# Measured step costs in the planner of a two-layer RG-LRU / Gated DeltaNet trunk

## The chip, the core and the metric

The kernel runs on one core of a Trainium2 chip. The core has a matrix engine (TensorE, PE in the profile), a vector engine (VectorE, DVE), an activation engine (ScalarE, ACT), a general engine (GpSimd, POOL) and a queue that issues the transfers (SyncE, SP). Each engine works through its own list of instructions in order; semaphores hold an instruction until what it reads is there. The metric is the device time of one execution in microseconds; the median of several runs is quoted.

## The reference

A sequence of 2048 frames of width 1024 passes two layers and a final norm, all in 32-bit floats.

```python
c_act = silu(c)
for i in range(2):
    shift, scale, gate = split(c_act @ ada_w[i] + ada_b[i])
    h = rmsnorm(x, norm_g[i]) * (1 + scale) + shift
    out = rglru_block(h) if i == 0 else gated_deltanet_block(h)
    x = x + gate * out
return rmsnorm(x, final_g)

# rglru_block: proj = h @ in_w (1024 -> 2048), causal conv of 4 taps, two gates by 8 block matmuls
#   (128x128), log_a = -8 * r * softplus(-lam), b = sqrt(1 - a^2) * i * x, scan h_t = a_t h_{t-1} + b_t,
#   y = scan * silu(zg), out = y @ out_w
# gated_deltanet_block: proj = h @ in_w (q, k, v, z of 8 heads x 128, and a, b), conv of 4 taps and SiLU
#   on q, k, v, l2norm of q and k, then per head, in chunks:
#   T = (I + strict lower of (beta k k^T * decay))^-1
#   v_new = T (beta v) - T (beta k exp(g)) S;  o = (q exp(g)) S + attn v_new
#   S = S * e_last + k_dec^T v_new
#   o = rmsnorm(o) * silu(z), out = o @ out_w
```

## The kernel before

**Tiling.** Frames are taken in two units `u` of 1024, each in two tiles `i` of 512 (`TC`). The hidden activations lie with channels on partitions. Every large product keeps 32-bit precision with three fast passes: each factor is split into a rounded part and the rest (`hh`/`hl` for activations, `whi`/`wlo` for weights), and `hi*hi + hi*lo + lo*hi` is accumulated. One job (`job`, through `products`, L668) is thus 24 matmuls of 128x128 by 512 columns into one bank of PSUM; `mm` is the bank of such a job, `mmo` that of an output projection.

**Stages.** The stages follow one another with some overlap. By the first and last matmul of each in the trace, in microseconds of the span: layer 1's input projection of unit 0 from 36 to 265 and of unit 1 to 476, with the conv (`convolve`, L746 to L769), the gates (`gates_thread`, L798 to L849) and the scan beside it; layer 1's output projection to 668; layer 2's input projection of unit 0 to 1217 and of unit 1 to 1734, with the work of the heads beside it; then layer 2's output projection with the final norm. In unit 0 of each layer the low part of a weight panel is made on GpSimd (`panels_thread`, L650) and kept in HBM; in unit 1 it is read back (L637).

**Layer 2, head by head.** A job's result is copied out (`extend`, L730), filtered by one step on GpSimd (L997) and three on VectorE (`taps`, L718), passed through tanh (L1009) and a multiply (L1014) and becomes `kt`, `qt` or `vt`. TensorE then transposes `kt` (`pk`, L1135), forms `pkk` (L1169) and `pqk` (L1257). `inverses_thread` inverts the 32x32 diagonal blocks on VectorE with 31 pairs of dependent small steps (`ttmp`, L1292, and `tblk`, L1295); `levels_thread` puts the blocks together with small matmuls (`px`, `pr`, L1334 to L1373). `recurrence_thread` goes through 8 chunks of 128 frames a unit and head. Each chunk is a chain over three engines: `pp` (two products with the state, L1412 and L1413), `zt` on VectorE (L1421), `py` (L1429), `yt` on ScalarE (L1435), `pS` (L1441, L1442), `state` on VectorE (L1454), and then `pp` of the next chunk. PE fills the time between with matmuls of the projection jobs.

**What sets the order.** The order on every engine is written by a planner inside the kernel when it is built, the class `Weave`. Each piece of work is a Python generator (a thread) with a priority. Before each step it yields the engine that the step needs, how long the step takes and, if wanted, a latency until its result may be used; it also yields events and buffer slots to wait for. `run` keeps a clock for each engine (`free`), takes the thread whose next step can start first (ties by priority), writes that step's instructions, and moves the clocks on. The clocks are the planner's own estimates; the chip knows only the order that they lead to and the semaphores. The jobs of the projection have the last priority, 9, and recurrences the first, 0. Transfers have an estimated speed, and `MARGIN` (2.4 us) is added behind some of them. In the text below, "planned" means by these clocks.

```python
LAG = {"pe": 0.2, "act": 0.3, "dve": 0.3, "pool": 0.2}           # latency where a step gives none
STT, EV, CP, TR, MM, M4 = 0.665, 0.605, 0.48, 0.109, 0.2163, 0.218
...
    self.free[w[0]] = t + w[1]
    th.t = t + w[1] + (w[2] if len(w) > 2 else self.LAG[w[0]])
```

`MM` is the planned time of one 512-column matmul in layer 2 and in both output projections; the jobs of layer 1 are given 0.2275.

## Time and profile before

| What | Value |
|---|---|
| median of 3 runs | 1935.67 us (1934.42 to 1940.69) |
| span of the profiled execution | 1937.1 us |
| PE busy / DVE busy / ACT busy / POOL busy | 1844.0 / 1471.2 / 1048.2 / 654.8 us |
| mean granted clock of TensorE | 0.984 |

The span is the time from the first to the last instruction of one profiled execution; the page shows no other time of that execution, and its span is 1.4 us above the median of the runs. A line of a group of instructions names the source line, the engine, the operation, what is written and read, the count, the busy time and the mean duration. A line of a wait names who waited for whom, the time in total, how often, and the longest. In a table of stretches, "PE busy (x)" is busy time and number of instructions, "PEclk" the share of TensorE's full clock that was granted. `PEld` is the load of a matmul's weights.

### The profile page before, as it was taken

To read this page: it belongs to the slowest core of one execution; us is meant where nothing else is said; L and a number is where in the kernel's file an instruction comes from. 1 tells how busy PE (TensorE), PEld (TensorE's weight loads), DVE (VectorE), ACT (ScalarE), POOL (GpSimd) and SP (SyncE) were. 2 spreads that over 40 slices of the span, in tenths; PEclk is the share of its full clock that TensorE was granted. 3 is DMA by queue.
4 is the path that set the end of the run, shared out by engine and by line. 5 is a ranking of instruction groups with operands and counts; after the bars stand their busy time and mean duration, and the time that the engine had idled before them with its cause. 6 is when DMAs were issued, how large, how long until landed. Compare 5 with 4: busy or idle time off the path is not lost.

```text
span 1937.1 us, 31289 instructions
## 1 busy us (share of the span) xinstructions
PE 1844.0 (95%) x10286; PEld 1503.9 (78%) x10286; DVE 1471.2 (76%) x3175; ACT 1048.2 (54%) x2587; POOL 654.8 (34%) x1116
## 2 busy tenths in 40 slices
PE   6999999999899999898999999999999999999998
PEld 3787778878688877677787877788888888888887
DVE  6898998887544668869888896769777878886653
ACT  3666677667212345375565663565666656654321
POOL 3344542223100235345445543333332334411110
PEclk9999999999899999999999998999999999999999
DMA  8476746554578735446676565555365555687751
GB/s 320 116 219 189 223 138 220 175 167 138 169 204 236 208 106 145 128 111 160 166 186 141 138 158 150 149 156 158 102 163 143 140 140 139 155 246 207 230 161 66
DMA packets 511723, 322.77 MB, mean 167 GB/s; under 512 B 371268, under 2 KB 439236, under 8 KB 511560
## 3 DMA queue, kind: packets, MB, share of 16 engines
q1 hardware_dynamic: 511560, 320.77, 59.1%
q8 instruction: 81, 1.33, 0.3%
q14 instruction: 82, 0.67, 0.1%
HBM read 219.93 MB, written 100.73 MB: 166 GB/s over the span
## 4 chain that ended last, share of the span: by engine, by line
PE 61%; DVE 20%; DMA 6%; issue 4%; ACT 4%; SPq 3%; POOL 2%; DVEq 0%; POOLq 0%; ACTq 0%
PE mm L668 31%; PE mmo L668 16%; DVE xf L718 2%; DVE ttmp L1292 2%; DVE tblk L1295 2%; PE pg L807 1%; PE py L1429 1%; PE pp L1412 1%; PE pS L1442 1%; PE pqk L1257 1%; PE pS L1441 1%; PE pp L1413 1%; PE pkk L1169 1%; DVE xf L756 1%; DMA raw<-in_w 1%
## 5 line engine op out<-in xcount | busy, mean ns | idle before, releaser
L718 DVE SCALAR_TENSOR_TENSOR xf<-xe,cw_s,xf 128x512 f32<-128x512 f32 x288 | 224.9, 784 | 20.6 <-POOL xf L997 18.1
L650 POOL TENSOR_TENSOR wlo<-raw,whi 128x1024 fp32r<-128x1024 f32 x48 | 120.9, 2519 | 143.6 <-ACT whi L644 115.4
L1292 DVE TENSOR_TENSOR ttmp<-blk,tblk 128x60 f32<-128x60 f32 (+24 forms) x496 | 125.4, 253 | 16.6 <-DMA blk<-blk_d 5.4
L1295 DVE TENSOR_TENSOR tblk<-tblk,ttmp 128x60 f32<-128x60 f32 (+24 forms) x496 | 124.8, 252 | 10.7
L644 ACT CAST whi<-raw 128x1024 fp32r<-128x1024 f32 x96 | 100.2, 1044 | 50.3 <-DMA raw<-in_w 44.5
L668 PE MATMUL mmo<-oh,yh 128*128 128x512 f32 x256 | 102.1, 399 | 4.8 <-ACT oh L907 4.8
L668 PE MATMUL mm<-hh_('in2', 0)_5342,whi 128*128 128x512 f32 x256 | 105.3, 411 | 0.0
L668 PE MATMUL mm<-hh_('in2', 0)_5437,whi 128*128 128x512 f32 x256 | 105.3, 411 | 0.0
L668 PE MATMUL mmo<-ol,yh 128*128 128x512 f32 x256 | 102.2, 399 | 3.0 <-DVE ol L909 3.0
L668 PE MATMUL mm<-hh_('in2', 0)_5342,wlo 128*128 128x512 f32 x256 | 104.7, 409 | 0.0
L668 PE MATMUL mm<-hl_('in2', 0)_5343,whi 128*128 128x512 f32 x256 | 104.7, 409 | 0.0
L668 PE MATMUL mm<-hl_('in2', 0)_5438,whi 128*128 128x512 f32 x256 | 104.1, 407 | 0.0
L668 PE MATMUL mm<-hh_('in2', 1)_12030,wlo 128*128 128x512 f32 x256 | 104.1, 407 | 0.0
L668 PE MATMUL mm<-hl_('in2', 1)_12219,whi 128*128 128x512 f32 x256 | 104.0, 406 | 0.0
L668 PE MATMUL mm<-hh_('in2', 0)_5437,wlo 128*128 128x512 f32 x256 | 103.9, 406 | 0.0
L668 PE MATMUL mm<-hh_('in2', 1)_12218,whi 128*128 128x512 f32 x256 | 103.6, 405 | 0.0
L668 PE MATMUL mm<-hh_('in2', 1)_12030,whi 128*128 128x512 f32 x256 | 103.5, 404 | 0.0
L668 PE MATMUL mm<-hl_('in2', 1)_12031,whi 128*128 128x512 f32 x256 | 103.3, 403 | 0.0
L668 PE MATMUL mm<-hh_('in2', 1)_12218,wlo 128*128 128x512 f32 x256 | 103.2, 403 | 0.0
L668 PE MATMUL mmo<-ol,oh 128*128 128x512 f32 (+1 forms) x264 | 103.1, 391 | 0.0
L668 PE MATMUL mmo<-oh,ol 128*128 128x512 f32 (+1 forms) x264 | 103.1, 391 | 0.0
L668 PE MATMUL mmo<-oh,oh 128*128 128x512 f32 (+1 forms) x264 | 103.0, 390 | 0.0
(331 smaller groups left out, 5649.8 us busy)
## 6 DMA issues: line engine op xcount, KB each, us to landing
raw<-in_w SPq DMA_DIRECT2D x96, 512.0 KB, 4.2
araw<-in_ada_w SPq DMA_DIRECT2D x32, 512.0 KB, 4.3
xt<-x_d SPq DMA_DIRECT2D x32, 512.0 KB, 4.9
xt_d<-xb SPq DMA_DIRECT2D x192, 64.0 KB, 2.4
xk<-xt_d SPq DMA_DIRECT2D x24, 512.0 KB, 6.1
xt<-in_x SPq DMA_DIRECT2D x16, 512.0 KB, 4.4
ada<-in_ada_w SPq DMA_DIRECT2D x16, 512.0 KB, 8.5
y_d<-tz SPq DMA_DIRECT2D x32, 256.0 KB, 3.2
```

Source lines behind the costliest of these rows:

```text
L644: act.copy(hi, raw)
L650: pool.tensor_tensor(lo, raw, f(hi), ALU.subtract)
L668: pe.matmul(pt, lhsT=lhs[a][:, k, :], rhs=rhs[b][:, k, :], start=(k == 0 and n == 0), stop=(k == KT - 1 and n == 2))
L718: dve.scalar_tensor_tensor(xf, xe[:, 1 + j:1 + j + TC], wc[:, j:j + 1], xf, ALU.mult, ALU.add)
L756: dve.scalar_tensor_tensor(xf[:, 3:TC], pt[:, j:j + TC - 3], wc[:, j:j + 1], xf[:, 3:TC], ALU.mult, ALU.add)
L807: pe.matmul(pg, lhsT=a[:, g, :], rhs=b, start=(q == 0), stop=(q == 2))
L1169: pe.matmul(pkk[:, b, :], lhsT=kc, rhs=kc, start=True, stop=True)
L1257: pe.matmul(pqk[:, b, :], lhsT=kt[:, b * P:(b + 1) * P], rhs=qt[:, b * P:(b + 1) * P], start=True, stop=True)
L1292: dve.tensor_tensor(tmp, blk[:, j, j + 1:32].unsqueeze(2).to_broadcast([P, r, c_]), t[:, j, 0:c_].unsqueeze(1).to_broadcast([P, r, c_]), A ...
L1295: dve.tensor_tensor(t[:, j + 1:32, 0:c_], t[:, j + 1:32, 0:c_], tmp, ALU.subtract)
L1412: pe.matmul(pp[:, 0, :], lhsT=kc, rhs=S_, start=True, stop=True)
L1413: pe.matmul(pp[:, 1, :], lhsT=qc, rhs=S_, start=True, stop=True)
```

## The change

Only the planner's numbers and rules change; every step still issues the same instructions with the same operands, and no buffer, slot, event or priority is touched. On each engine the same instructions stand in another order; ScalarE alone has ten more loads of a function table, 63 for 53, which the build puts in where the function set changes from one instruction to the next. There are five parts.

1. **Durations.** Most steps get another duration, given as the distance from the start of one step to the start of the next on that engine.
2. **Latencies.** The latency behind a step becomes 0.2 us for PE, 0.128 for ScalarE, 0.113 for VectorE and 0.034 for GpSimd, in place of 0.2, 0.3, 0.3 and 0.2. Own latencies of steps (0.13, 0.27, 0.0 and others) go, apart from a few with `MARGIN`.
3. **Weights.** When a thread comes to PE from another engine or from a wait, and PE would otherwise go straight on, 0.12 us is added.
4. **Tables.** A step on ScalarE that needs the set of exp and tanh, or that of sqrt, names it; 1.28 us is added where the planner's present set is the other. Before, every sqrt was simply given 3.1 us.
5. **Steps that exclude each other.** A VectorE step marked `dve2` that would start while a GpSimd step marked `pool2` is planned to run starts when that one ends, and the reverse.

```diff
+LAG = {"pe": 0.2, "act": 0.128, "dve": 0.113, "pool": 0.034}
+WEIGHTS = 0.12
+TABLE = 1.28
+SHARED = {"dve2": "pool2", "pool2": "dve2"}
...
-    LAG = {"pe": 0.2, "act": 0.3, "dve": 0.3, "pool": 0.2}
...
+        self.held = {"dve2": [], "pool2": []}
+        self.table = "exp"
...
-        return max(th.t, self.free.get(w[0], 0.0))
+        free = self.free.get(w[0].rstrip("2"), 0.0)
+        if w[0] == "pe" and th.last != "pe" and th.t > free - 0.1:
+            return max(free, th.t + WEIGHTS)
+        return max(th.t, free)
+
+    def engine(self, th, t, kind, dur, lag=None, table=None):
+
+        e = th.last = kind.rstrip("2")
+        if table is not None and table != self.table:
+            t, self.table = t + TABLE, table
+        if kind in SHARED:
+            for a, b in self.held[SHARED[kind]][-6:]:
+                if a <= t < b:
+                    t = b
+            self.held[kind].append((t, t + dur + (0.08 if e == "dve" else 0.0)))
+        self.free[e] = t + dur
+        th.t = t + dur + (LAG[e] if lag is None else lag)
...
+            if t > th.t and not isinstance(w, tuple):
+                th.last = None
...
-                self.free[w[0]] = t + w[1]
-                th.t = t + w[1] + (w[2] if len(w) > 2 else self.LAG[w[0]])
+                self.engine(th, t, *w)
...
-    STT, EV, CP, TR, MM, M4 = 0.665, 0.605, 0.48, 0.109, 0.2163, 0.218
+    STT, EV, CP, TR, MM, M4 = 0.665, 0.605, 0.48, 0.109, 0.228, 0.224
...
-                    yield "pool", 2.3
+                    yield "pool2", 2.39
                     pool.tensor_tensor(lo, raw, f(hi), ALU.subtract)
...
-            yield "dve", STT, 0.13 if j < 3 else 0.27
+            yield "dve2", 0.663
             dve.scalar_tensor_tensor(xf, xe[:, 1 + j:1 + j + TC], wc[:, j:j + 1], xf, ALU.mult, ALU.add)
...
-        yield "dve", 0.7
+        yield "dve2", 0.599
         xl = tile_([P, TC], "xr", "xl", F32R)
...
-        yield "act", 3.1
+        yield "act", 0.54, LAG["act"], "sqrt"
         act.activation(tr, tr, AF.Sqrt, scale=-0.25)
...
-        yield "dve", EV
+        yield "dve2", 0.604
         r = tile_([P, TC], kind + "t", kind + "t")
...
-            dur = 0.065 + r * c_ / 960.0
-            yield "dve", dur, 0.13
+            dur = 0.075 + r * c_ / 960.0
+            yield "dve2", dur
...
-                    yield "dve", 0.27
+                    yield "dve", 0.265
                     zt = tile_([P, P], "zt", "zt")
...
-                yield "act", 0.16
+                yield "act", 0.18
                 yt = tile_([P, P], "yt", "yt")
...
-                yield "dve", 0.27
+                yield "dve", 0.258
                 if first:
                     dve.tensor_copy(out=S_, in_=pS[:, 0, :])
```

The other threads change in the same way. The built orders are compared below at three places; lines of the changed kernel are 17 higher than the same lines before.

The first place is on PE in layer 2, unit 0: the two transposes of `kt` (`pk`, four instructions each) that stand at 802 and 807 us of the profiled execution. Before, one matmul of a job stands between them:

```order
L668 MATMUL mm<-hl_('in2', 0)_5343,whi 128x512
L1135 MATMUL pk<-ident,kt 128x128 x4
L668 MATMUL mm<-hh_('in2', 0)_5342,wlo 128x512
L1135 MATMUL pk<-ident,kt 128x128 x4
L668 MATMUL mm<-hh_('in2', 0)_5437,whi 128x512
L668 MATMUL mm<-hl_('in2', 0)_5438,whi 128x512
```

Now the second of them stands here, thirty rows behind the first:

```order
L685 MATMUL mm<-hh_('in2', 0)_5455,whi 128x512
L685 MATMUL mm<-hl_('in2', 0)_5456,whi 128x512
L685 MATMUL mm<-hh_('in2', 0)_5455,wlo 128x512
L685 MATMUL mm<-hh_('in2', 0)_5455,whi 128x512
L685 MATMUL mm<-hl_('in2', 0)_5456,whi 128x512
L1380 MATMUL px_7011<-tf,ac 64x64 x8
L1152 MATMUL pk<-ident,kt 128x128 x4
L685 MATMUL mm<-hh_('in2', 0)_5455,wlo 128x512
```

Eleven matmuls of the next job and two sets of small products (`pr` and `px`) moved in between the two transposes.

The second place is on PE in layer 2, unit 1, inside the chain of chunks of one head. Before, `py` of a chunk is followed by four matmuls of a job, then `pS`, then five, then `pp` of the next chunk:

```order
L668 MATMUL mm<-hh_('in2', 1)_12030,wlo 128x512
L668 MATMUL mm<-hh_('in2', 1)_12030,whi 128x512
L668 MATMUL mm<-hl_('in2', 1)_12031,whi 128x512
L668 MATMUL mm<-hh_('in2', 1)_12030,wlo 128x512
L1441 MATMUL pS<-yt,kd 128x128
L1442 MATMUL pS<-yt,at 128x128
L668 MATMUL mm<-hh_('in2', 1)_12030,whi 128x512
L668 MATMUL mm<-hl_('in2', 1)_12031,whi 128x512
L668 MATMUL mm<-hh_('in2', 1)_12030,wlo 128x512
L668 MATMUL mm<-hh_('in2', 1)_12030,whi 128x512
L668 MATMUL mm<-hl_('in2', 1)_12031,whi 128x512
L1412 MATMUL pp<-state_106,kt 128x128
```

Now, for the same head:

```order
L1446 MATMUL py<-zt,ac 128x128
L685 MATMUL mm<-hh_('in2', 1)_12131,wlo 128x512
L685 MATMUL mm<-hh_('in2', 1)_12131,whi 128x512
L685 MATMUL mm<-hl_('in2', 1)_12132,whi 128x512
L1458 MATMUL pS<-yt,kd 128x128
L1459 MATMUL pS<-yt,at 128x128
L685 MATMUL mm<-hh_('in2', 1)_12131,wlo 128x512
L685 MATMUL mm<-hh_('in2', 1)_12131,whi 128x512
L685 MATMUL mm<-hl_('in2', 1)_12132,whi 128x512
L1429 MATMUL pp<-state_106,kt 128x128
```

One matmul of a job moved out of the first interval and two out of the second.

The third place is on ScalarE in layer 1, around one sqrt (L830 before, L847 now). Before:

```order
L752 COPY edge_123<-mm 128x3
L830 ACT_TABLE_LOAD
L830 ACTIVATE tg<-tg 128x512
L783 ACT_TABLE_LOAD
L783 ACTIVATE tz<-mm 128x512
L857 ACTIVATE tg<-pg,gb_s 128x512
```

Now:

```order
L769 COPY edge_123<-mm 128x3
L847 ACT_TABLE_LOAD
L847 ACTIVATE tg<-tg 128x512
L874 ACT_TABLE_LOAD
L874 ACTIVATE tg<-pg,gb_s 128x512 x2
```

The load after the sqrt now stands ahead of a gate's tanh rather than of the `z` path's. In all, 31 loads ahead of a sqrt stand there now, and 26 before.

Counted over PE's list in the same way: from the last matmul of a job to the `pg` that depends on it (layer 1, unit 0), the median distance is 61 matmul slots before and 99 now; from a `k` job to its `pk` in the second half of layer 2's unit 0, 52 before and 62 now; from a `q` job to its `pqk` there, 57 and 85. In layer 2's unit 1 the same two distances are 41 and 40, and 46 and 46. A slot is one 512-column matmul, or one small 32-bit product of 128 columns. In the chain of chunks the intervals from the first `pp` to `py`, from `py` to the first `pS` and from the first `pS` to the next `pp` were counted, in slots that stand between, the second product of a pair included. Of some 180 such intervals in unit 1, 2 had room for no more than three other matmuls before, and 51 have now; in unit 0, 12 of 150 before, and 64 now.

More of the change, by code (lines that the diff above doesn't have):

```diff
@@ L63, in __init__ @@
     def __init__(self, gen, prio, t):
-        self.gen, self.prio, self.t, self.want = gen, prio, t, None
+        self.gen, self.prio, self.t, self.want, self.last = gen, prio, t, None, None
 class Weave:
     SEEN = 0.92
-    LAG = {"pe": 0.2, "act": 0.3, "dve": 0.3, "pool": 0.2}
     def __init__(self):
         self.free = dict.fromkeys(("pe", "act", "dve", "pool", "sp", "dma"), 0.0)
+        self.held = {"dve2": [], "pool2": []}
+        self.table = "exp"
         self.threads = []
@@ L312, in first_small_thread @@
         w.set(ev("c"))
-        yield "dve", 1.57
+        yield "dve", 1.6
         for k in range(KT):
@@ L385, in columns_thread @@
         dve.tensor_scalar(sp2, sp2, 2.0, None, ALU.mult)
-        yield "act", 0.2
+        yield "act", 0.111, LAG["act"], "exp"
         act.activation(aexp, alog_s, AF.Exp)
-        yield "dve", 0.1
+        yield "dve", 0.085
         dve.tensor_scalar(aexp, aexp, -1.0, None, ALU.mult)
@@ L451, in scale_thread @@
         put("tt", ttok)
-        yield "pool", 0.75, MARGIN / 2 if late else 0.2
+        yield "pool", 1.2, MARGIN / 2 if late else 0.2
         rs = tile_([P, 1], "rs", "rs")
@@ L558, in split_thread @@
         ttok = yield slots[tag]
-        yield "act", 0.665
+        yield "act", 0.711
         h = tile_([P, TC], tag, "h")
@@ L683, in job @@
         pt = ps.tile([P, TC], F32, tag=bank, name="mm")
-        yield from products(pt, (hi, lo), h, (lambda k: ev("split", (name, i), k)), 0.2275 if layer == 1 else MM)
+        yield from products(pt, (hi, lo), h, (lambda k: ev("split", (name, i), k)))
         if all(q != p for q, _ in jobs[n + 1:]):
@@ L722, in extend @@
         if g == 0:
-            yield "pool", 0.1
+            yield "pool", 0.101
             pool.memset(xe[:, 0:4], 0.0)
@@ L726, in extend @@
             yield ev("carry", key, g - 1)
-            yield "pool", 0.14
+            yield "pool", 0.299
             pool.tensor_copy(out=xe[:, 0:4], in_=carry)
-        yield "act", CP
+        yield "act", 0.484
         act.copy(xe[:, 4:4 + TC], pt)
         put(bank, mtok)
-        yield "pool", 0.14, 0.0
+        yield "pool", 0.279
         pool.tensor_copy(out=carry, in_=xe[:, TC:TC + 4])
@@ L739, in convolve @@
     def convolve(xf, pt, mtok, wc, bias, edge, key, g, bank):
-        yield "act", 0.66 if bias is not None else 0.57, 0.0
+        yield "act", 0.681
         if bias is None:
@@ L795, in gates_thread @@
             w.set(ev("lasthalves"))
-        yield "act", CP
+        yield "act", 0.521
         xh = tile_([P, TC], "xh", "xh", F32R)
         act.copy(xh, xf)
-        yield "dve", 0.7
+        yield "dve2", 0.599
         xl = tile_([P, TC], "xr", "xl", F32R)
@@ L832, in gates_thread @@
             yield ev("hcar", n, u * NTC + i - 1)
[L833 removed]
+        yield "dve2", 0.603
         dve.tensor_tensor(ti, ti, tr, ALU.mult)
         put("tg", rtok)
[L836 removed]
+        yield "dve2", 1.19
         init = 0.0 if u + i == 0 else hcar[:, n:n + 1]
@@ L952, in residual1_thread @@
         row = yield ev("gate", 0, d)
-        yield "dve", EV
+        yield "dve", 0.616
         dve.tensor_tensor(pt, pt, row[:, d * TC:(d + 1) * TC], ALU.mult)
-        yield "dve", EV
+        yield "dve", 0.606
         dve.tensor_tensor(xr, pt, xr, ALU.add)
@@ L1187, in key_thread @@
         for b in range(TB):
-            yield "act", 0.295, 0.0
+            yield "act", 0.298
             act.activation(kd[:, b, :], kd[:, b, :], AF.Copy, scale=ec[:, b, P - 1:P])
-        yield "pool", 0.16
+        yield "pool", 0.343
         pool.tensor_tensor(nk, nk, rr, ALU.mult)
```

221 lines of the change are left out of this document (109 added, 112 removed).

## The prediction, as it was made before the run

> **What bounds the kernel now.** I read the busy times first, then the table of stretches, then what PE waits for in each stretch, and last the timeline around the longest wait.
>
> ```profile
> PE 1844.0 (95%) x10286; PEld 1503.9 (78%) x10286; DVE 1471.2 (76%) x3175; ACT 1048.2 (54%) x2587; POOL 654.8 (34%) x1116
> ```
>
> PE has 1937.1 - 1844.0 = 93 us without work. The change adds and removes no work on PE, so it can only move this idle time and the clock that goes with it. The stretches say where that is:
>
> ```profile
> core 0: us, PE busy (x) PEld busy (x) DVE busy (x) ACT busy (x) POOL busy (x), PEclk, DMA share, GB/s
> 60.00:270.00 210.00, 196.34 (x839) 156.65 (x837) 190.22 (x278) 139.24 (x210) 100.40 (x86) 0.98 0.64 188
> 270.00:490.00 220.00, 219.26 (x950) 176.53 (x950) 182.21 (x276) 156.60 (x215) 66.53 (x60) 0.99 0.55 171
> 490.00:720.00 230.00, 221.10 (x953) 175.76 (x952) 127.87 (x185) 62.01 (x98) 38.36 (x55) 0.98 0.64 183
> 720.00:1000.00 280.00, 257.02 (x1666) 212.97 (x1664) 225.51 (x550) 159.49 (x493) 132.92 (x241) 0.98 0.58 149
> 1000.00:1240.00 240.00, 222.78 (x1429) 182.87 (x1428) 198.53 (x537) 139.38 (x424) 109.21 (x186) 0.97 0.60 153
> 1240.00:1720.00 480.00, 477.10 (x3212) 398.65 (x3212) 371.76 (x1051) 293.18 (x927) 160.95 (x389) 1.00 0.57 146
> ```
>
> Layer 2's unit 0 (720 to 1240) leaves PE idle for 23.0 + 17.2 = 40.2 us; unit 1 (1240 to 1720), which does nearly the same per head, for 2.9. The granted clock is 0.98 and 0.97 in unit 0 and 1.00 in unit 1; if the missing clock were all lost, it would cost 0.02 x 280 + 0.03 x 240 = 12.8 us. Layer 1's unit 0 (60 to 270) has 13.7 us idle and 0.02 x 210 = 4.2 us of clock. What differs between the units of layer 2 is the GpSimd step that makes the low half of a weight panel, L650:
>
> ```profile
> 720.00:1000.00 280.00, 41.51 (x17) 0.98 0.58 149
> 1000.00:1240.00 240.00, 26.84 (x11) 0.97 0.60 153
> 1240.00:1720.00 480.00, 0.00 (x0) 1.00 0.57 146
> ```
>
> The timeline shows what it does to VectorE (three engines, each in its own order):
>
> ```profile
> 801.49 2.89 POOL L650 TENSOR_TENSOR wlo<-raw,whi 128x1024 fp32r<-128x1024 f32 x1 [3.40 <-ACT whi L644]
> ...
> 802.08 2.40 DVE L1292 TENSOR_TENSOR ttmp<-blk,tblk 128x75 f32<-128x75 f32 x1
> ...
> 805.32 0.23 DVE L1292 TENSOR_TENSOR ttmp<-blk,tblk 128x70 f32<-128x70 f32 x1
> ...
> 806.26 0.68 DVE L1014 SCALAR_TENSOR_TENSOR kt<-tt,xf 128x512 f32<-128x512 f32 x1
> ...
> 807.00 0.66 PE L1135 MATMUL pk<-ident,kt 128*128 128x128 f32 x4 [3.89 <-DVE kt L1014]
> ```
>
> A small step that takes 0.23 us when alone takes 2.40 while L650 runs, and ends with it. `kt` stands behind it in VectorE's list, and PE, which has `pk` next in its own, stands still for 3.89 us. The old planner had no rule for this. All waits of PE over 1.5 us in unit 0 of layer 2, and those of layer 1's unit 0 and of the switch to layer 1's output projection that matter (who waits for whom, us in total, times, the longest):
>
> ```profile
> PE pk L1135 <- DVE kt L1014: 7.6, 4, 3.9
> PE pp L1412 <- DVE state L1454: 6.4, 7, 1.8
> PE py L1429 <- DVE zt L1421: 5.3, 4, 1.9
> PE pqk L1257 <- DVE qt L1014: 3.3, 1, 3.3
> PE px L1334 <- DVE tf L1327: 3.3, 5, 1.6
> PE pqk L1257 <- DVE tblk L1295: 2.1, 1, 2.1
> PE px L1363 <- POOL rq L243: 2.1, 1, 2.1
> PE pqk L1257 <- DVE ttmp L1292: 1.9, 1, 1.9
> PE pS L1441 <- ACT yt L1435: 1.8, 2, 1.5
> PE pp L1412 <- DVE ttmp L1292: 1.6, 1, 1.6
> PE pk L1135 <- DVE ttmp L1292: 1.6, 1, 1.6
> ```
>
> ```profile
> PE pg L807 <- DVE xl L801: 6.4, 6, 1.9
> ```
>
> ```profile
> PE mmo L668 <- ACT oh L907: 4.8, 2, 3.6
> PE mmo L668 <- DVE ol L909: 3.0, 2, 2.2
> ```
>
> **The change, part by part.**
>
> *Exclusion and measured durations, unit 0 of layer 2.* Nothing makes the collisions fewer: L650 still runs as often, and a VectorE step that meets it still waits. What the planner gains is that it knows of the delay, and puts a projection matmul where PE would have stood. The order shows it: a `k` job is 52 slots ahead of its `pk` in the median before and 62 now, a `q` job 57 and 85 ahead of `pqk`. Ten slots of 0.23 us (the rows of the next part) are 2.3 us, more than the mean `pk` wait of 7.6 / 4 = 1.9. I take all waits of `pk` and `pqk` as gone: 7.6 + 1.6 + 3.3 + 2.1 + 1.9 = 16.5 us. Their share of the clock goes with them, 12.8 x 16.5 / 40.2 = 5.3. Of the 5.4 us of `px` I take half, 2.7, since nothing in the order says more. Together -24.5. The bounds are 0 (the collisions come elsewhere) and -53.0 (all idle time and all clock).
>
> *Shorter latencies, the chain of chunks.* One hop of unit 1, PE's rows and then VectorE's:
>
> ```profile
> 1534.76 0.39 PE L1412 MATMUL pp<-state,kt 128*128 128x128 f32 x2
> ...
> 1535.90 0.39 PE L668 MATMUL mm<-hh_('in2', 1)_12030,wlo 128*128 128x512 f32 x1
> 1536.13 0.27 PE L1429 MATMUL py<-zt,ac 128*128 128x128 f32 x1
> ```
>
> ```profile
> 1535.48 0.34 DVE L1421 SCALAR_TENSOR_TENSOR zt<-pp,eg,vn 128x128 f32<-128x128 f32 x1
> ```
>
> A slot lasts 0.23 us. `zt` ends at 1535.82, and `py` starts 0.31 us later. With one matmul less in between it would have 0.08 us to spare, and any VectorE step in the way makes PE wait. Some 49 intervals of unit 1 and 52 of unit 0 are now that short. Each can cost nothing (VectorE happens to be free) or, as long as only this hop is late, a slot. That bounds each unit at 0 and 49 x 0.23 = 11 or 52 x 0.23 = 12 us. I take 0.1 us each, nearer the lower end because the hop shown would still have been in time: +5 in each unit. The 15.1 us that the chain waits in unit 0 today (6.4 + 5.3 + 1.8 + 1.6) I leave as they are.
>
> *Layer 1's unit 0.* A `pg` stands 99 slots behind its job, in place of 61. The 38 slots more are 8.7 us, and its longest wait was 1.9, so the 6.4 us go, with their share of the clock, 4.2 x 6.4 / 13.7 = 2.0: -8.4. VectorE is busy for 190 of these 210 us, so the delay can come out at another matmul; the bounds are 0 and -17.9 (13.7 + 4.2).
>
> *The switch to layer 1's output projection.* The 7.8 us of `oh` and `ol` follow a transfer, two steps and the freeing of a tile; nothing in the change bears on that. I take 0, with bounds of -8 and +8, as much again.
>
> *Table loads.* Ten more on ScalarE:
>
> ```profile
> L830 ACT ACT_TABLE_LOAD x26 | 33.4, 1283 | 0.5
> ```
>
> 10 x 1.283 = 12.8 us, in a stage (60 to 490) in which ScalarE is busy for 139.2 + 156.6 of 430 us. The 134 us of idle time cover it; without that cover it is +12.8. I take 0. [...]
>
> *The rest* (small durations, POOL's latency, the 0.12 us for weights) moves steps by less than a slot each; it is in the counts above.
>
> The sum is -24.5 + 5 + 5 - 8.4 = -22.9: a span of 1914.2 us. The runs' median stands 1.4 us below the profiled span (1935.67 for 1937.1), so **1913 us**.
>
> **The rivals.**
>
> *The cushion goes (slower).* The old planner gave a matmul of layer 2 0.2163 us where a slot lasts 0.23. On the chip every planned distance on PE was thus 6% longer than planned, a hidden margin for VectorE and ScalarE, and most VectorE steps had a latency of 0.3 us where 0.113 stands now. The new numbers take both away everywhere in layer 2, not only in the chain. For it: unit 1 waits 2.9 us with that margin although VectorE is busy for 372 of 480 us. Against it: `pk` and `pqk` of unit 1 keep their distance (41 and 40 slots, 46 and 46). If unit 1 then loses half of what unit 0 loses now per microsecond, 480 x 0.5 x 53 / 520 = 24, and unit 0 gains nothing, the time is 1935.7 + 24 = 1960. It decides once the new waits exceed the 33 us that the other terms save, 0.33 us on each of the 101 shortened intervals; one slot each isn't enough, so the waits must spread beyond the chain.
>
> *The collisions only move (no change).* When L650 starts depends on when its panel lands, which the planner only guesses; a start that is 2 us off puts the 2.4 us of the VectorE step at 802 on another one than planned. Then PE still waits, elsewhere, and gains of 10 meet losses of 10: 1936. For it speaks the 3.40 us that POOL waited before the L650 shown. Against it, the distances grew for all consumers in unit 0, whichever step is hit. [...]
>
> *Everything goes (much faster).* PE waits no longer in 60 to 270 and 720 to 1240: 17.9 + 53.0 = 71 us, 1865. For it: unit 1 shows that PE can run so. Against it: the shorter hops.
>
> **How the numbers follow.** The forecast, with its own range of 1890 to 1929, gets 0.44; everything goes 0.16; no change 0.15; slower 0.25. A change of under 0.3% (5.8 us) can't be told from none here. So faster 0.60, same 0.15, slower 0.25. The range goes from 1872, which leaves out the last part of the case in which all waits go, to 1955, which leaves out the worse part of the slower one.
>
> **What would show it.** Right: PE's idle time in layer 2's unit 0 falls from 40 to about 22 us while VectorE's steps under L650 stay as long; no `pk` or `pqk` among the waits over 2 us; `pg` gone from the waits; some 5 us of new waits of `py`, `pS` and `pp` in unit 1. Wrong: unit 1's idle time over 15 us, or unit 0's as before with other names on the waits.

## The result: 3.1% slower, and the profile after

| | before | changed |
|---|---|---|
| median | 1935.36 us (4 runs, 1934.42 to 1940.69) | 1997.97 us (4 runs, 1997.38 to 1998.57) |
| span of the profiled execution | 1937.1 us | 1996.9 us |
| last matmul of layer 1's input projection, unit 0 / unit 1 | 265 / 476 | 283 / 498 |
| length of layer 1's output projection | 192 | 197 |
| length of layer 2's input projection, unit 0 / unit 1 | 549 / 518 | 553 / 546 |
| length of layer 2's output projection | 195 | 196 |

The ratio is 1.031, with a 95% interval of 1.030 to 1.033. The lengths of the stages are worked out from the last matmul of each in the two traces. The loss stands in two places: 22 us by the end of layer 1's input projection, and 32 us in layer 2's. Another 5 us lie in layer 1's output projection.

The busy times of the page after, to be read against those of before:

```profile
span 1996.9 us, 31308 instructions
...
PE 1868.4 (94%) x10286; PEld 1521.0 (76%) x10286; DVE 1452.5 (73%) x3175; ACT 1056.0 (53%) x2597; POOL 646.7 (32%) x1116
```

PE does the same 10286 instructions, and is without work for 1996.9 - 1868.4 = 128.5 us, 35.4 more than before. Its mean granted clock fell from 0.984 to 0.965: at full clock, 1996.9 x 0.035 = 70 us are missing, against 1937.1 x 0.016 = 31. That is 39 us more of missing clock. The two overlap, since part of the low clock falls on time in which PE stands still: the added 35.4 and 39 come to 74 us where the span grew by 60. VectorE is busy for 19 us less than before. The table of stretches, same columns as before:

```profile
60.00:270.00 210.00, 188.52 (x776) 150.62 (x776) 173.49 (x250) 136.15 (x196) 91.90 (x77) 0.93 0.59 175
270.00:490.00 220.00, 213.60 (x928) 172.86 (x928) 179.16 (x288) 163.49 (x224) 54.07 (x64) 0.98 0.53 171
490.00:720.00 230.00, 219.35 (x925) 172.00 (x924) 118.12 (x167) 60.90 (x81) 33.62 (x43) 0.98 0.62 178
720.00:1000.00 280.00, 261.60 (x1550) 215.52 (x1550) 215.50 (x540) 147.91 (x457) 132.52 (x229) 0.96 0.57 151
1000.00:1240.00 240.00, 215.80 (x1432) 179.40 (x1431) 188.69 (x522) 136.12 (x432) 106.06 (x197) 0.93 0.60 150
1240.00:1720.00 480.00, 467.27 (x3109) 389.19 (x3108) 363.43 (x1008) 289.96 (x909) 165.16 (x373) 0.99 0.52 135
```

By these rows PE idles for 21.5 us of layer 1's unit 0 (13.7 before), 18.4 + 24.2 = 42.6 us of layer 2's unit 0 (40.2) and 12.7 us of its unit 1 (2.9). The clock is down to 0.93 in two stretches. What PE waits for in layer 1's unit 0 (60 to 283 us; who waits for whom, us in total, times, the longest):

```profile
PE mm L685 <- DVE xf L773: 13.6, 3, 6.1
PE mm L685 <- DVE tz L802: 7.1, 2, 6.5
PE pg L824 <- DVE xl L818: 0.5, 2, 0.3
```

The `pg` waits are down from 6.4 us to 0.5, and a projection job now waits for a PSUM bank that the conv (L773) or the `z` path (L802) frees late. The same view for layer 2's unit 0 (695 to 1247 us):

```profile
PE px L1351 <- DVE tz L1042: 8.4, 1, 8.4
PE pk L1152 <- DVE ttmp L1309: 4.7, 2, 4.3
PE py L1446 <- DVE zt L1438: 4.3, 6, 1.1
PE px L1380 <- DVE ac L1374: 3.8, 1, 3.8
PE pS L1458 <- ACT yt L1452: 3.2, 7, 0.8
PE pp L1429 <- DVE state L1471: 2.7, 6, 0.8
PE px L1380 <- ACT tf L1369: 2.6, 1, 2.6
```

`pqk` has left the top of the list, `pk` has one long wait left, and `px` has taken over.

### The profile page after: what moved, and what is told of

The parts are those of the page before. It is cut to its first block, busy times and chain, and to the rows that moved or that the text cites. A ratio compares the mean times of both kernels' runs of the same rounds, so it can differ in the third digit from the quotient of the medians.

```text
span 1996.9 us, 31308 instructions
## 1 busy us (share of the span) xinstructions
PE 1868.4 (94%) x10286; PEld 1521.0 (76%) x10286; DVE 1452.5 (73%) x3175; ACT 1056.0 (53%) x2597; POOL 646.7 (32%) x1116
## 4 chain that ended last, share of the span: by engine, by line
PE 52%; DVE 17%; DMA 12%; ACT 6%; SPq 5%; issue 4%; POOL 3%; DVEq 0%; POOLq 0%; ACTq 0%
PE mm L685 27%; PE mmo L685 12%; DMA x_d<-xr 3%; DVE xf L735 2%; DVE ttmp L1309 2%; DMA raw<-in_w 2%; DVE tblk L1312 2%; PE py L1446 1%; PE pp L1429 1%; SPq L527 1%; PE pg L824 1%; PE pS L1458 1%; PE pS L1459 1%; PE pp L1430 1%; DMA araw<-in_ada_w 1%
## 5 line engine op out<-in xcount | busy, mean ns | idle before, releaser
L685 PE MATMUL mm<-hh_('in2', 0)_5455,whi 128*128 128x512 f32 x256 | 106.3, 415 | 0.5 <-DVE tz L1042 0.5
L685 PE MATMUL mm<-hl_('in2', 0)_5456,whi 128*128 128x512 f32 x256 | 105.1, 411 | 0.0
L685 PE MATMUL mm<-hh_('in2', 1)_11914,wlo 128*128 128x512 f32 x256 | 104.8, 409 | 0.0
L685 PE MATMUL mm<-hh_('in2', 0)_5455,wlo 128*128 128x512 f32 x256 | 104.6, 408 | 0.0
L685 PE MATMUL mm<-hh_('in2', 1)_11914,whi 128*128 128x512 f32 x256 | 104.4, 408 | 0.0
L685 PE MATMUL mm<-hh_('in2', 1)_12131,whi 128*128 128x512 f32 x256 | 104.2, 407 | 0.0
L685 PE MATMUL mm<-hh_('in2', 0)_5284,whi 128*128 128x512 f32 x256 | 103.5, 404 | 0.6 <-DVE tf L1356 0.6
L685 PE MATMUL mm<-hh_('in2', 1)_12131,wlo 128*128 128x512 f32 x256 | 103.9, 406 | 0.0
L685 PE MATMUL mm<-hl_('in2', 1)_11915,whi 128*128 128x512 f32 x256 | 103.8, 406 | 0.0
L685 PE MATMUL mm<-hl_('in2', 1)_12132,whi 128*128 128x512 f32 x256 | 103.4, 404 | 0.0
```

The costliest lines, as they stand in the source:

```text
L685: pe.matmul(pt, lhsT=lhs[a][:, k, :], rhs=rhs[b][:, k, :], start=(k == 0 and n == 0), stop=(k == KT - 1 and n == 2))
```

## The experiments

Two quantities go with each run. One is its time. The other can be had without a chip: the planner's own clocks say when PE has no step, and the sum of those gaps is called the **planned idle time** here. It is 41.8 us for the kernel before and 86.6 for the changed one.

### The first four: one part of the change taken back

Four theories stood against each other. In the first, layer 1 loses by ScalarE's order: before, the conv's two ScalarE steps that read the PSUM bank (L763 and L767) stood together, since the first had a latency of 0.0 of its own; with 0.128 a sqrt and its table load get in between. That is the case at 19 of 32 convs in the changed kernel and at none before. The timeline around the longest wait of layer 1 shows it:

```profile
255.58 0.77 ACT L763 ACTIVATE xf<-mm,cb_s,cw_s 128x509 f32<-128x509 f32 x1
256.36 1.28 ACT L847 ACT_TABLE_LOAD   x1
257.65 0.63 ACT L847 ACTIVATE tg<-tg 128x512 f32<-128x512 f32 x1
258.19 0.15 ACT L767 COPY edge<-mm 128x6 f32<-128x6 f32 x1
258.31 0.69 DVE L851 TENSOR_TENSOR tg<-tg 128x512 f32<-128x512 f32 x1 [1.35 <-ACT tg L847]
258.35 1.28 ACT L800 ACT_TABLE_LOAD   x1
...
259.65 0.60 ACT L800 ACTIVATE tz<-mm 128x512 f32<-128x512 f32 x1
...
261.41 0.68 DVE L802 SCALAR_TENSOR_TENSOR tz<-tz,mm 128x512 f32<-128x512 f32 x1
...
262.14 0.79 PE L685 MATMUL mm<-hh_('in1', 0)_209,whi 128*128 128x512 f32 x1 [6.49 <-DVE tz L802]
...
262.73 0.63 PE L685 MATMUL mm<-hl_('in1', 0)_210,whi 128*128 128x512 f32 x1
263.16 0.63 PE L685 MATMUL mm<-hh_('in1', 0)_209,wlo 128*128 128x512 f32 x1
```

The last two rows also show the second price of such a wait: the matmuls behind it start 0.43 us apart, where a slot lasts 0.23. The other theories were the cushion (the slower rival of the prediction), the exclusion rule, and layer 1's numbers as a whole.

**The two steps joined again.**

```diff
-        yield "act", 0.681
+        yield "act", 0.681, 0.0
```

> The changed kernel with one number altered: the first of the two ScalarE steps with which the conv of layer 1 reads its PSUM bank (L763) gets its old own latency of 0.0 back, so that the second one (L767) follows it in the planner's list. In the built order something stands between the two at 9 of 32 convs, never a sqrt, where it is 28 of 32 in the changed kernel, 19 of them a table load and a sqrt. Theory of the split (the loss of layer 1, 22 us from the first matmul to the last of its input projection, comes from a sqrt that was let in between the two, so that VectorE frees the bank late and PE waits for it): the mean time from the start of L763 to the end of the third tap falls from 6.4 us to below 5, PE's wait of mm for xf (20.0 us) to below 5, and the time to 1976-1984. Theory of the cushion (all of the loss lies in planned distances of PE that are now exact) and theory of the exclusion rule: 1995-2000, since neither is touched.

Measured: 1995.54 us, 1.031 times the kernel before (1.029 to 1.033). The bank was indeed held for less: from the start of L763 to the end of the third tap the mean is 4.5 us and not 6.4 (4.7 before the change). The largest waits of PE in the whole span show what became of it:

```profile
PE pg L824 <- DVE xl L818: 17.3, 7, 9.1
...
PE mm L685 <- DVE xf L773: 6.8, 4, 4.2
```

The wait for `xf` fell from 20.0 us to 6.8, and `pg`, which had lost its waits by the change, waits for 17.3. The split is there, and the bank is freed as early as its theory said, but taking it away moves the wait. The 2.4 us saved lie within the spread of this kernel's own runs (1992.8 to 1999.0). The theory of the split had expected 1976 to 1984, the other two 1995 to 2000.

**Layer 1's own numbers as before**, in four threads, for instance:

```diff
-        yield "act", 0.54, LAG["act"], "sqrt"
+        yield "act", 3.1, 0.3
         act.activation(tr, tr, AF.Sqrt, scale=-0.25)
```

> The changed kernel with the step times and latencies of before in four threads of layer 1 (conv, z path, gates, gate; no exclusion and no table rule there), everything else as changed. Any theory in which layer 1's loss has its cause in layer 1's own numbers: the input projection of layer 1 ends at 476-482 us in place of 498, and the time falls by 16-25 us to 1973-1982, with layer 2 as slow as in the changed kernel (30-36 us more than before). If layer 1's loss came from the rules that still hold there (weights, exclusion of the conditioning steps, the other threads' times): 1990 or more. If layer 2's loss hung on how layer 1 ends: under 1965.

Measured: 1986.43 us (1.026; 1.024 to 1.028). Layer 1's input projection ends at 480 us, as expected, but its output projection takes 206 us in place of 197, and half of the 18 us gained is lost there. The time stays 4 us above what the theories of layer 1's own numbers had allowed.

**The planned matmul of layer 2 as before.**

```diff
-    STT, EV, CP, TR, MM, M4 = 0.665, 0.605, 0.48, 0.109, 0.228, 0.224
+    STT, EV, CP, TR, MM, M4 = 0.665, 0.605, 0.48, 0.109, 0.2163, 0.218
```

> The changed kernel with the planned matmul of layer 2 and of both output projections at 0.2163 us again (and 0.218 for the small products that name it), layer 1 at 0.228 as changed. Theory of the cushion, the slower rival of the prediction: layer 2's 33 us come back and the time is 1960-1970, with unit 1's projection stretch of layer 2 near 520 us in place of 547. Theory that layer 2 lost by its step latencies or by the exclusion rule: 1990-2002.

Measured: 2005.29 us (1.035; 1.033 to 1.037), slower than the changed kernel. Unit 1 takes 576 us, not 520. The cushion had expected 1960 to 1970: giving the margin back doesn't give the time back.

**Without the exclusion rule.**

```diff
-SHARED = {"dve2": "pool2", "pool2": "dve2"}
+SHARED = {}
```

> The changed kernel without the rule that VectorE and GpSimd steps exclude each other; durations, latencies, table rule and weights as changed. Theory of the exclusion rule (steps planned later than the chip needs them push the conv and the chain back): 1940-1965. Theory of the split: the built order has something between the conv's two ScalarE steps at 17 of 32 places, 9 of them a sqrt with its table load, so about half of layer 1's 22 us comes back: 1985-1990. Theory of the cushion: 1994-2002, or slower, since the GpSimd collisions in layer 2 are no longer planned for.

Measured: 1994.84 us (1.030; 1.028 to 1.033). The planned idle time falls to 29.7 us, and the waits that the changed kernel shows in layer 1 are gone from the plan. The chip makes others of them:

```profile
PE pg L824 <- DVE xl L818: 12.4, 13, 3.4
PE pk L1152 <- DVE kt L1031: 10.8, 7, 2.6
...
PE pp L1429 <- DVE state L1471: 9.3, 6, 2.6
```

These are the waits of the kernel before, enlarged. The theory of the exclusion rule missed by 30 us, that of the split by 5; the time is the one that the cushion had expected (1994 to 2002).

### Four more, in both directions

**The old default latencies in the changed kernel.**

```diff
-LAG = {"pe": 0.2, "act": 0.128, "dve": 0.113, "pool": 0.034}
+LAG = {"pe": 0.2, "act": 0.3, "dve": 0.3, "pool": 0.2}
```

> The changed kernel with the default latencies of before (0.3 us for ScalarE and VectorE, 0.2 for PE and GpSimd); durations, the exclusion rule, weights and tables as changed. After the first four runs neither the planned matmul, nor the exclusion rule, nor the split conv alone carries the loss of 62 us. [...] Theory that the durations or the other rules did it: 1990-2005.

Measured: 2059.56 us (1.064; 1.062 to 1.067). By the theory of the latencies, 0.3 us is a margin for what the planner doesn't know, and both layers gain; the author's estimate for it, 1945 to 1970 us, missed by 90. Longer planned latencies did not protect the chain of chunks. Its `py`, `pp` and `pS` wait 26, 24 and 27 times, where they wait 6, 9 and 8 times in the changed kernel:

```profile
PE py L1446 <- DVE zt L1438: 12.6, 26, 1.3
...
PE px L1351 <- DVE ttmp L1309: 10.7, 1, 10.7
PE pp L1429 <- DVE state L1471: 10.8, 24, 0.7
PE pS L1458 <- ACT yt L1452: 10.0, 27, 0.4
```

The planner's clocks say why: 207.5 us of planned idle time, with one gap of 14.3 us in front of a `px`. A longer planned latency only becomes a margin while the planner still has matmuls of a job to put into it. Where it has none, the chain stands in PE's list without a matmul of a job between its steps. That is so at 81 places here, 41 in the changed kernel and 14 before, and PE waits at 74 of the 81, for 31 us in all.

**Layer 2's step times as before**, in all threads of the heads (out of the exclusion rule, too), for instance:

```diff
-                yield "dve", 0.258
+                yield "dve", 0.27, 0.3
                 if first:
                     dve.tensor_copy(out=S_, in_=pS[:, 0, :])
```

> The changed kernel with the step times and latencies of before in all threads of layer 2's heads (copies, conv, keys, queries, values, inverses, levels, recurrence, outputs), which are then outside the exclusion rule too; layer 1, weight panels, splitting and norms as changed, and the rules too. If layer 2's 33 us come from its own numbers: layer 2's projection of both units takes 1060-1075 us in place of 1099, and the time is 1962-1975. If from the planned matmul, the weights rule or the shared steps (panels, splitting): 1990 or more.

Measured: 1976.94 us (1.022; 1.020 to 1.024), the largest gain by a part taken back, and 2 us outside the range of the theory that layer 2's loss lies in its own numbers. That theory's stage didn't come: layer 2's input projection takes 1090 us in place of 1099, where 1060 to 1075 were expected. The output projection takes 190 in place of 196, and most of the rest is layer 1's output projection.

**Without the rule for weights.**

```diff
-WEIGHTS = 0.12
+WEIGHTS = 0.0
```

> The changed kernel with 0.0 in place of 0.12 us for a thread that comes to PE from elsewhere. The rule puts a small product behind one more matmul at most, so if it matters at all it protects the chain: every theory under test expects 1992-2004, and under 1985 would mean that the rule itself puts PE's order wrong.

Measured: 1992.28 us (1.030; 1.029 to 1.032). Layer 1's input projection ends at 482 us, 16 earlier than in the changed kernel, its output projection takes 8 us less, and layer 2 takes 16 us more. The 6 us of the sum, within what every theory had expected, hide moves of 24 and 16.

**The exclusion rule alone, in the kernel before.** The rule and the same marks, with the old numbers:

```diff
-        return max(th.t, self.free.get(w[0], 0.0))
+        return max(th.t, self.free.get(w[0].rstrip("2"), 0.0))
...
+                if w[0] in SHARED:
+                    for a, b in self.held[SHARED[w[0]]][-6:]:
+                        if a <= t < b:
+                            t = b
...
```

> The kernel before with the exclusion rule alone (the same steps marked, old durations, old latencies, no weights, no table rule). Theory that the rule is good and the shorter latencies and durations spoil it: unit 0 of layer 2 loses its waits of pk and pqk, 1915-1930. Theory that the rule itself does harm (it moves a step behind a GpSimd step that on the chip comes at another time): 1940-1960. Theory that collisions only move: 1930-1942.

Measured: 2015.45 us (1.042; 1.039 to 1.045), outside all three. By itself the rule costs 81 us, more than the whole change. PE's largest waits are those for PSUM banks in layer 1 and the same `px` as in the changed kernel:

```profile
PE mm L677 <- DVE xf L765: 17.6, 5, 7.1
PE mm L677 <- DVE tz L794: 16.9, 5, 8.0
...
PE px L1343 <- DVE tz L1034: 8.0, 2, 7.2
```

The planned idle time is 151.4 us. This led to the theory of planned waiting: where the planner's clocks leave PE without a step, the order leaves it without one on the chip. In the changed kernel the gaps of the plan can be laid beside those of the trace, each in front of the same instruction (start of the gap and its length, us):

```
              layer 1: mm                                       layer 2: pk      px2       px2       px
planned       146 5.0   176 2.6   222 2.9   235 6.5   291 5.2   775 3.6   908 2.6   1037 3.0   1146 4.1
on the chip   157 6.1   191 3.6   242 3.9   256 6.5   316 5.3   827 4.3   970 3.8   1107 2.6   1227 8.4
```

Here `px2` is the second `px` of a head (L1380). These are all waits of PE over 2.5 us on the chip from 60 us to the end of layer 2's unit 0. So the long waits of the changed kernel up to there aren't accidents of the chip: they stand in the plan. It doesn't hold the other way for all. Two more planned gaps of this size came out shorter, one of 2.6 us at a `pg` (no wait on the chip) and one of 3.2 at a `pr` (1.6 us); and in unit 1 the chip has waits of 2.7 us at a `pqk` and at a `pr` that the plan doesn't have. The kernel before has no planned gap over 1 us between 60 us and the end of layer 1's unit 0, and two of 7.0 and 3.7 us at the switch to the output projection.

### Margin or planned waiting

**Old latencies, no exclusion rule** (the edits of two runs above together):

> The changed kernel with the default latencies of before (0.3, 0.3, 0.2, 0.2) and without the exclusion rule: the run with the latencies of before, minus the rule. By the planner's own clocks PE then stands idle for 144 us, against 42 before, 87 in the changed kernel, 208 with old latencies and the rule, and 30 without the rule alone. Theory of planned waiting (where the planner's clocks leave PE without a step, the order leaves PE without one on the chip too, so a dearer plan is a slower kernel): 2005-2040, slower than the changed kernel. Theory of the latency cushion (0.3 us protects the order from what the planner doesn't know, and only together with the rule was it too much): 1940-1970.

Measured: 2063.42 us (1.067; 1.065 to 1.068). Planned waiting had the sign right and the size too small (it allowed 2040); the cushion missed by 93 us.

**Short default latencies alone, in the kernel before** (the four numbers of `LAG`):

> The kernel before with the four default latencies of the change (0.128 for ScalarE, 0.113 for VectorE, 0.034 for GpSimd); durations, own latencies and everything else as before. Planned idle of PE 28 us against 42 before. Theory of planned waiting: no slower than before, 1920-1940. Theory of the latency cushion: its loss in the middle of the chain costs 20 us or more, 1950-1980.

Measured: 1955.89 us (1.011; 1.010 to 1.013). Here the cushion was right and planned waiting wrong.

**The planned matmul alone, in the kernel before** (0.228 and 0.224):

> The kernel before with the planned matmul of layer 2 and the output projections at 0.228 us and the small products at 0.224, as in the change, and nothing else. This is the slower rival's first half by itself. Planned idle 37 us against 42. Theory of planned waiting: 1925-1942. Theory of the cushion (6 per cent of hidden margin in layer 2): 1950-1965.

Measured: 1980.92 us (1.025; 1.023 to 1.027): 46 us, more than either theory allowed, by the one number whose return to the changed kernel had cost 7.

**The exclusion rule in the choice.** The changed kernel with the delay counted when the next step is chosen:

```diff
         free = self.free.get(w[0].rstrip("2"), 0.0)
+        if w[0] in SHARED:
+            t = max(th.t, free)
+            for a, b in self.held[SHARED[w[0]]][-6:]:
+                if a <= t < b:
+                    t = b
+            return t
```

> The changed kernel with the exclusion rule moved: the delay counts when the planner chooses the next step (a step that would have to wait lets another go first), where the changed kernel chooses first and then moves the chosen step, and its engine, back. All numbers as changed. Planned idle of PE 69 us against 87. Theory of planned waiting: two thirds of the difference come back as in the earlier pairs, 1980-1990. Theory that the rule is right and only its place was wrong: 1930-1950. Theory that VectorE's order is not what binds: 1993-2002.

Measured: 1972.5 us (1.020; 1.017 to 1.023), the fastest kernel with all the new numbers, but between the ranges of two theories. Whether the rule's place did it is taken up below.

For the short latencies and the planned matmul in the kernel before, the cushion had the sign right twice and the size once, and planned waiting was wrong both times; in the changed kernel the cushion missed by 35 us or more wherever it expected a gain. What all had in common was that every altered kernel took 20 us or more longer than the kernel before. So the next runs altered numbers by amounts that mean little or nothing. Their expectations add a theory, the **tuned draw**: each set of numbers is one throw, and the order before was a good one.

### Numbers without a meaning

**A planned matmul of 0.2170 in place of 0.2163 us, in the kernel before.**

```diff
-    STT, EV, CP, TR, MM, M4 = 0.665, 0.605, 0.48, 0.109, 0.2163, 0.218
+    STT, EV, CP, TR, MM, M4 = 0.665, 0.605, 0.48, 0.109, 0.217, 0.218
```

> The kernel before with a planned matmul of 0.2170 us in place of 0.2163, a change of 0.3 per cent that no account of margins can give a price (0.7 ns on each of 24 matmuls a job). From the first tiles of layer 2 on, the built order is still another one on every engine. Theory of the cushion (the time follows the margin that the planned matmul hides): 1932-1940. Theory of planned waiting: planned idle 59 us against 42, so about 10 us slower, 1940-1950. Theory of the tuned draw (the planner's result jumps with any of its numbers, the order before is a picked good one, and any other numbers cost some ten us whatever they mean): 1945-1975.

Measured: 1973.51 us (1.021; 1.019 to 1.023). A change of 0.3% in one number costs 40 us, as only the tuned draw had allowed. Layer 1's input projection is the same to 2 us. Layer 2 shows the picture that was to be explained, more idle time and a lower clock in all three stretches:

```profile
720.00:1000.00 280.00, 254.51 (x1531) 209.71 (x1530) 218.76 (x535) 147.75 (x450) 122.38 (x222) 0.94 0.58 145
1000.00:1240.00 240.00, 214.97 (x1409) 176.44 (x1407) 184.83 (x506) 133.89 (x413) 100.07 (x187) 0.96 0.58 149
1240.00:1720.00 480.00, 474.46 (x3165) 396.74 (x3165) 371.95 (x1043) 298.71 (x939) 173.36 (x392) 0.99 0.53 137
```

**More margin, 0.2105.**

> The kernel before with a planned matmul of 0.2105 us: more cushion, 9 per cent in place of 6. Theory of the cushion: no slower than before, 1920-1938. Theory of planned waiting: planned idle 79 us against 42, 1950-1965. Theory of the tuned draw: 1945-1975, as for any other number.

Measured: 1985.29 us (1.027; 1.024 to 1.030), above the ranges of all three theories. **Half of the margin, 0.2220.**

> The kernel before with a planned matmul of 0.2220 us, half of the way to the 0.228 that cost 46 us. Theory of the cushion: half of it, 1952-1964. Theory of planned waiting: planned idle 38 us against 42, 1930-1940. Theory of the tuned draw: anywhere in 1945-1985, with no order between 0.217, 0.222 and 0.228.

Measured: 1958.84 us (1.013; 1.011 to 1.016), within the ranges of the cushion and of the tuned draw. The five kernels that differ in nothing but the planned matmul (the last also in `M4`) read:

```
planned matmul, us   0.2105   0.2163   0.2170   0.2220   0.2280
time, us             1985.3   1935.4   1973.5   1958.8   1980.9
```

There is no order in this. More margin isn't better and less isn't worse; the cushion falls as a cause. The kernel before is the best of the five, and what sets it apart from its neighbour at 0.2170 isn't any meaning of 0.0007 us.

**Both old margins of layer 2 in the changed kernel** (the old step times of the heads and the old planned matmul):

> The changed kernel with the numbers of before in layer 2 as far as they go together: the step times of the heads' threads and the planned matmul of 0.2163 us. Of the change, layer 2 then keeps only the weights rule and the numbers and marks of the weight panels, the splitting and the norms. Theory of the cushion: layer 2's 33 us come back whole, 1960-1968, better than the 1977 with the step times alone. Theory of planned waiting: planned idle 92 us against 57 with the step times alone, 1985-2000. Theory of the tuned draw: near 1977, since layer 2 gets one more order that nobody picked.

Measured: 1992.9 us (1.030; 1.027 to 1.033): 16 us slower than with the step times alone. The cushion had expected some 12 us faster, and the tuned draw about the same. Planned waiting, with 92 us of planned idle time for 57, had it right.

**The changed kernel with two of its numbers moved slightly**, down by 0.3%, and up by 0.6 and 0.3% (to 0.665 and 0.2287). The planned matmul of layer 1's jobs stays. The edit down is:

```diff
-            yield "dve", 0.661
+            yield "dve", 0.659
...
-    STT, EV, CP, TR, MM, M4 = 0.665, 0.605, 0.48, 0.109, 0.228, 0.224
+    STT, EV, CP, TR, MM, M4 = 0.665, 0.605, 0.48, 0.109, 0.2273, 0.224
```

> The changed kernel with two of its new numbers moved by 0.3 per cent: the conv's tap 0.659 in place of 0.661 us (layer 1) and the planned matmul of layer 2 and of the output projections 0.2273 in place of 0.2280; rules and everything else as changed. Neither number means anything else than before. Planned idle 106 us against 87. Theory of the tuned draw (each set of numbers is one throw; the order before was a good one of its kind, the changed one an ordinary or bad one): another time in 1965-2005, with both layers' stage lengths moved by several us either way. Theory that the new rules and numbers themselves place the steps badly: the same 1993-2003, stage by stage (layer 1's input projection ends at 498 +-4, layer 2 takes 1295 +-6). Theory of planned waiting: 2005-2015.

> The same on the other side: the conv's tap 0.665 and the planned matmul 0.2287. Planned idle 79 us against 87. Theory of the tuned draw: another time in 1965-2005, not tied to the one of the run with 0.659 and 0.2273. Theory that the rules and numbers themselves do it: 1993-2003, stage by stage. Theory of planned waiting: 1988-1996.

Measured: 2000.56 us (1.034; 1.033 to 1.036) with the smaller numbers and 1975.3 us (1.022; 1.019 to 1.024) with the larger. The first looks like the changed kernel in its time only: layer 1's input projection ends at 482 us and not at 498, and layer 2's unit 1 takes 562 and not 546. The second ends that projection at 486 us and takes 536 for unit 0 of layer 2, which is less than the kernel before takes, and 564 for unit 1. So the changed kernel's stages aren't fixed by its rules and numbers either. Both times lie in the wide range of the tuned draw (1965 to 2005). Planned waiting missed both, by 4 and 13 us.

## Why the prediction was wrong

**What the runs settle.** The planner is a list scheduler whose result can jump when one of its numbers moves by 0.3%. The five kernels with the planner of before and a few numbers altered take 1956 to 1985 us, with a mean of 1971; three with the changed planner take 1975, 1998 and 2001. The 62 us have no price list by parts: taken back one at a time in the changed kernel, the parts of this change gave 2.4 (split), 11.5 (layer 1's numbers), -7.3 (planned matmul), 3.1 (exclusion), -61.6 (latencies), 21.0 (layer 2's step times) and 5.7 us (weights), and two that go together gave 5.1 where their sum would be 13.7. Layer 2's loss lies within what meaningless numbers make of it: from the end of layer 1 to the last matmul it takes 1262 us before, 1273 to 1306 in the four kernels whose planned matmul was altered, and 1295 in the changed kernel. Of the 22 us that layer 1's input projection loses, the changed kernel's two neighbours lose only 6 and 10.

**What they leave open.** The means of the two groups, 1971 and 1991, are 20 us apart, with five and three members; whether the change carries a loss of its own beside the lost order can't be said from so few. The eight other kernels with the changed planner and its short latencies, in which a part was taken back or the rule moved, average 1990 us as well; that speaks for a loss of its own of some 20 us, but doesn't show it. Differences of 2 to 6 us between single kernels, as those of the split, the rule and the weights, say nothing either way. Why the order before is better than its neighbours isn't shown either. That the exclusion rule in the choice gains 25 us isn't shown, since one of the changed kernel's own neighbours gains 23. Planned idle time goes with the time (correlation 0.86 over the 20 kernels measured), but mostly through its three extremes, the kernels over 2010 us; without them it is 0.69, and it misjudged the short latencies, 0.2280 and the kernel without the rule.

The forecast was 1913 us, in a range of 1872 to 1955; 1998 us were measured. Now the prediction's steps, one by one.

- *Unit 0 of layer 2, -24.5 us.* Only a part of the named waits went: all waits of `pk` and `pqk` in unit 0 came to 17.9 us (16.5 of them counted on) and come to 8.0 now, while unit 1 has 6.8 us of them in place of 1.1. The time didn't go with them; unit 0's stage took 4 us more. The stretches show 42.6 us of idle time for 40.2, under other names (`px` above all: 16.1 us for 5.4), which the prediction had listed as the sign that it was wrong. The failed step is "I take all waits of `pk` and `pqk` as gone" as a gain: it took the rest of the old order as given, and the whole order was new. What the runs showed in its place is that another order brings waits of its own: with the planned matmul at 0.2170 and nothing else altered, the same two stretches idle for 50.5 us.
- *The clock, 5.3 and 2.0 us.* Mis-sized, and in the wrong direction. The prediction took the clock's loss as a share of idle time. In the stage of unit 0 the trace has half the clock for 61 us now and 27 before, at nearly the same idle time (42.6 and 38.8 by matmuls); in layer 1's unit 0 it is 31 us for 7. In the stage of unit 0, waits of 3 us and more come to 16.4 us now and to 7.2 before, and the longest stretch of half clock (23.9 us) begins amid waits of 1.6 to 2.6 us among small products. What of that stretch is due to the waits and what to the small products, no run separates.
- *The chain of chunks, +5 us in each unit.* The sign is right in unit 1 and wrong in unit 0, and it isn't what unit 1 lost by. In unit 1's stage (1247 to 1794) the chain's three (`py`, `pS`, `pp`) wait for 4.7 us, where they had 2.8 in the same stage before (1217 to 1735); in unit 0 they fell from 15.8 to 11.6. Unit 1's stage idles for 18.0 us in place of 4.8. The longest waits are those of `pr` and `pqk`:

```profile
PE pr L1363 <- DVE tz L1042: 2.7, 1, 2.7
PE pqk L1274 <- DVE qt L1031: 2.7, 1, 2.7
PE px L1351 <- DVE tz L1042: 2.0, 1, 2.0
```

Besides, that stage has half the clock for 13.7 us in place of none, and 78 matmuls more than before, while unit 0's has 68 fewer: work moved from one stage to the next.

- *Layer 1's unit 0, -8.4 us.* The `pg` waits went, as said. The stage took 18 us more, by waits for PSUM banks that stand in the plan itself (21 us in 60 to 283). That the planner could plan to leave PE idle wasn't among the terms.
- *The switch to the output projection, 0 with bounds of 8.* Within its bounds: the stage took 5 us more. In the other runs it took 181 to 206, more than the bounds allow.
- *Table loads, 0.* Ten more loads were made, and some stand in the way of the conv. Joining the conv's steps took the sqrt out of there and gained 2.4 us, so the term is small, as said. In the traces of the kernel before and of the changed one, a load puts 1.30 us or more between the end of the step before it and the start of the step behind it.
- *The cushion goes, 1960.* Right on the sign, wrong on the reason. Its own number alone cost the kernel before 46 us, but so did 0.2170 (40) and 0.2105 (51), which have nearly the same cushion and more of it.
- *Everything goes, 1865.* Nothing speaks for it: PE's idle time rose by 35 us.
- *The collisions only move.* This half was right. Worked out over the trace, 198 marked VectorE steps began within a marked GpSimd step before, and 193 do now; VectorE's extra time in them is 127 us before and 105 now. A rule that only pays for a meeting in the plan hardly makes meetings fewer.

## What to carry to other kernels

Before you price a change to a planner, move one of its numbers by 0.3% and measure: that spread, here up to 40 us, is what a new order may cost, and a gain summed up from the waits of the old order counts for nothing below it. A fast order must be compared with several neighbours of the changed one, and not with a single one. And ask the planner first: a wait that stands in its own clocks can be seen before the chip is asked, and of the eleven longest in the changed kernel's plan behind 60 us the chip made nine. A plan without such waits is no promise, though: the kernel without the rule planned 30 us and took 1995.

## What the runs showed of the hardware

**A wait of PE costs more than itself.** Over the 20 profiles, from 30 us on, a gap of PE at full clock was followed within 5 us by half the clock in 124 of 125 cases when it was 3 us or longer, in 74 of 104 at 2 to 3 us, and in 120 of 347 at 1 to 2 us. So half the clock often followed gaps below 3 us, too. The half clock lasts 3.41 us or a multiple, but for the last one of a trace; the longest stretch is 37.5 us, in the run with the numbers moved down, and the changed kernel has one of 23.9 us from 1107.8, in which PE's list held 64 small products and three matmuls of a job.

**Which VectorE steps wait for GpSimd.** In the trace before, the 198 marked VectorE steps that began within a marked GpSimd step took 640 ns longer than alone, where that step had 1019 ns to go. The 99 unmarked ones in the same position that read PSUM (67) or are transposes (32) lasted as long as alone: 4 ns less in the mean, and 15 ns more at most. Unmarked steps weren't free of it as such: of nine small ones on `sp` and `gg` (L257, L258) in that position, eight took 0.3 to 2.2 us longer than alone.
